# Where the text puts the mixers of a two-layer backbone: whole, or in pieces between products

## The chip, the cores and the metric

One core of one Trainium2 chip runs the whole program. The metric is the device time of one execution in microseconds.

## What is computed

Two streams of 256 tokens with 1024 features, a context (`c`) and the latents (`x`), pass through two layers. Each layer first mixes tokens and then channels:

```python
u_x = modulate(h_x, norm1[layer], sh1_x, sc1_x)
u_c = modulate(h_c, norm1[layer], sh1_c, sc1_c)
mix_c, mix_x = token_mixers(u_c, u_x, need_ctx, ...)   # w_in, four mixers, w_out
h_x = h_x + g1_x * mix_x
...
f = swiglu(flat, ...) if layer % 2 == 0 else moe_swiglu(flat, ...)
```

`token_mixers` multiplies by `w_in` (1024 x 2992), gives groups of columns to four mixers, concatenates their 4 x 256 output columns and multiplies by `w_out`. The mixers are windowed attention (A), the gated delta rule in both directions (B), latent attention (C) and retention (D). The latents read the context's keys, values and states; the context never reads the latents. In the last layer the context is only needed for those, so it has no output projection and no channel mixing there. Layer 0 has a dense SwiGLU of 3584 hidden units for both streams, layer 1 the top two of eight experts for the latents alone.

## The kernel before

Long products (input projection, output projection, channel mixing) are made exact by parts: a weight block is loaded to `raw` (five buffers), ScalarE rounds it to `hi` (L200, L225), VectorE takes the rest as `lo` (L201, L226), and TensorE (PE) runs three matmuls for each pair of blocks (`mm3`, L183 to L185, into the tile `acc`). Activations are split in the same way once. Weight loads are issued on SP's queue (L193 for blocks of 512 columns, L212 for blocks of 256, L287 for the modulation).

The kernel is written as a text in program order. For each engine the scheduler takes, of the instructions that are ready, the one that stands first in that text; `soon()` (L162) counts its instructions as 6000 places earlier, and is put around the splits of weights, around what empties the accumulators and around norms. Each engine then runs its own list in that order. Buffers of the mixers are single or double, named by tags, so a later user waits for the earlier one.

The functions that the change touches or that its steps pass through:

- `proj` (L1175) is a generator of the input projection. Its groups are `g` (delta rule: a group of 272 columns and three pairs of feature blocks, followed by the short convolution), `r` (retention: two groups of 512 columns), `a` (latent attention's 416 columns, then windowed attention's 512). For the latents of layer 0 the order is `rga`, a step for `r`, one for `g`, two for `a`.
- `gdn` (L938) is the delta rule. It transposes keys and values (L946), forms the systems of all chunks (L987 to L999), sends them to DRAM and back so that the 16 x 16 blocks on the diagonals lie a block to a partition (L1001, L1013), inverts these by forward substitution on VectorE (L1018 on), sends the inverses through DRAM again (L1026, L1034, L1035), and then takes four chunks, two steps in each of two directions, each with `inverse` (L1028) and `scan` (L1089). Chunks of one direction depend on each other through a state.
- `ret` (L749), `mla` (L641) and `swa` are retention, latent and windowed attention. The three of them share two PSUM banks (thread `AT`), so they follow each other. `attend` goes head by head: scores, maximum, exponential, transposes, sum, scaling into the tile `mix`.
- `outproj` (L1280) transposes `mix` (tile `mixt`, L1289) and multiplies by `w_out`; `add_residual` adds the gated result to the stream (tile `rtmp`, L373, and L374, for channel mixing partly on GpSimd).
- `ffn` (L1304) is a generator of dense channel mixing; each of its seven steps is a block of 512 hidden units. `tick` runs steps of the modulation's products between long products; `put_fill` queues such steps, `need_mod` runs them out.
- `load_stream` issues the two loads of a residual stream.

The decay tables of the delta rule (`gdn_decay`, with additions on GpSimd at L932) are made by the projection's last use of its first group, not by `gdn`. The order of the work around the change is that of the lines L1386 to L1423: first all four mixers of the context, then the latents' projection with the context's output projection in it, then all four mixers of the latents, then channel mixing of the context and of the latents; and in layer 1 the context's short projection, its delta rule, and the rest of the latents' channel mixing.

Of the kernel before, what the change touches and what calls it, by code (L numbers as in the profile page):

```python
# [17 lines left out]
PSUM = bass.MemoryType.PSUM  # L18
# [52 lines left out]
def bc(ap, pos, n):  # L71
    """Broadcast a new free dimension of n elements at position pos of the pattern."""
    a = list(ap.ap)
    a.insert(pos, [0, n])
    return bass.AP(tensor=ap.tensor, offset=ap.offset, ap=a)
# [3 lines left out]
def tile_backbone(ctx: ExitStack, tc: tile.TileContext, x, ctxs, cT, w_mod, w_in, w_out, w_q_up, w_kv_up,  # L79
# [42 lines left out]
    class Thread:  # L122
        """The rotating buffers of one strand of work."""
# [11 lines left out]
    class Long(Thread):  # L135
        """the strand of the long products: two pairs of banks take turns as accumulators,
        and what is short goes to the pair that is not at work"""
# [24 lines left out]
    def soon():  # L162
        """for what feeds the long matrix products"""
        return tc.high_priority(offset=6000)
# [22 lines left out]
    def slabs(w2d, nk, ranges, r0=0, ticks=(), calls=None):  # L187
        """Yields, for each block of 128 rows, the two exact parts of the columns in the ranges."""
        for a in range(0, nk, 2):
            r = raw.tile([128, 2, 512], F32, name="raw", tag="raw")  # L190
            w = 0
            for c0, c1 in ranges:
                nc.sync.dma_start(r[:, :, w:w + c1 - c0], w2d[r0 + a * 128:r0 + a * 128 + 256, c0:c1].rearrange(  # L193
                    "(k p) c -> p k c", p=128))
                w += c1 - c0
            for j in range(2):
                hi = spl.tile([128, 512], F32R, name="hi", tag="hi")
                lo = spl.tile([128, 512], F32R, name="lo", tag="lo")
                with soon():
                    S.copy(hi[:, :w], r[:, j, :w])  # L200
                    V.tensor_tensor(lo[:, :w], r[:, j, :w], hi[:, :w].bitcast(F32), op=OP.subtract)  # L201
                yield a + j, hi[:, :w], lo[:, :w]
            if a // 2 in ticks:
                tick()
            if calls and a // 2 in calls:
                calls[a // 2]()

    def halfslabs(w2d, nk, c0, ticks=()):
        """the same for 256 columns from c0"""
        for a in range(0, nk, 4):  # L210
            r = raw.tile([128, 2, 512], F32, name="raw", tag="raw")
            nc.sync.dma_start(r.rearrange("p a (b c) -> p (a b) c", c=256),  # L212
                              w2d[a * 128:a * 128 + 512, c0:c0 + 256].rearrange("(k p) c -> p k c", p=128))
            for j in range(2):
                hi = spl.tile([128, 512], F32R, name="hi", tag="hi")
                lo = spl.tile([128, 512], F32R, name="lo", tag="lo")
                with soon():
                    tsplit(hi, lo, r[:, j])
                for i in range(2):
                    yield a + j * 2 + i, hi[:, i * 256:i * 256 + 256], lo[:, i * 256:i * 256 + 256]  # L220
            if a // 4 in ticks:
                tick()
# [5 lines left out]
    class Parts:  # L228
        """feature-major activations [128, 8 blocks, 256 tokens] in two exact parts, a tile for two blocks"""

        def __init__(self, tags=None):
            """tags: buffers of mixers that aren't at work, in place of the own ones"""
            self.t, self.tags = [], tags
# [19 lines left out]
    def silu2(dst, src, n):  # L253
        """dst = 2 silu(src)"""
# [11 lines left out]
    # ---- residual streams  # L266
# [9 lines left out]
    # ---- modulation  # L276
# [26 lines left out]
    def bank0(name):  # L303
        """the banks that nothing else uses at the start"""
        turns.append(turns.pop(0))
        return turns[-1].ps(name)
# [22 lines left out]
    class Fill:  # L329
        """steps of the modulation that go between the long products"""  # L330
# [32 lines left out]
    def gate_tile(l, kind, s, factor, apart=False):  # L363
        """factor times a gate, along the columns of every partition"""
# [11 lines left out]
    # ---- modulated RMS norm, feature-major, in two exact parts  # L376
# [48 lines left out]
    # ---- rotary embedding of token-major heads: returns the two addends  # L425
# [18 lines left out]
    def put_mix(s, t, k0):  # L444
        """the 256 columns, from 128 k0, of the concatenated mixer outputs of a token tile"""
# [4 lines left out]
    # ---- softmax attention shared by the windowed and the latent mixers  # L450
    def attend(th, tp, s, t, score_fn, nk, v_fn, scale, sink, k0):
        """score_fn(h) -> PSUM scores [128, nk]; v_fn(h, kt) -> [128 keys, 64]; tp: thread of the transposes"""
# [32 lines left out]
    # ---- mixer A  # L485
# [57 lines left out]
    # ---- mixer C  # L543
    STC = {}

    def mla_in(l, s, full, c0):
        """c0: column of the key latent in the projected group (query latent at 0 when full)"""
# [103 lines left out]
    # ---- mixer D  # L651
    STD = {}

    def ret_tables(l):
# [11 lines left out]
        for h in range(4):  # L666
            # one of the two factors is 1 everywhere; both directions count on the diagonal
# [5 lines left out]
        # per token decays, [tile, head, direction]: of the context into its state, of the latents from it  # L673
# [16 lines left out]
    def ret_in(s, full):  # L690
        """keys and values"""
# [33 lines left out]
    def ret_qg(s):  # L725
        """queries and gates"""
# [67 lines left out]
    def gn_out(th, s, oc, g, k0):  # L794
        """oc: [128, 2 tiles x 4 heads x 64]; oc / rms(oc) times the gates"""
# [19 lines left out]
    # ---- mixer B  # L815
# [5 lines left out]
    # a [128, 128] matrix takes 128 rows of 128 and 128 more, which makes its blocks of 16 on the diagonal  # L821
    # and those of the matrix that follows equally spaced
    PAD = 128 * 129
    def mats(t, q):
        """the four matrices of a chunk, rows first"""
        return dram(t, [[128, 128], [PAD, 4], [1, 128]], q * 4 * PAD)

    def blocks(t, a, b):
        """the blocks of 16 on the diagonals"""
# [4 lines left out]
    def conv(l, sq, f, src):  # L834
        """short convolution over the tokens and twice silu of a block of 128 features"""
# [25 lines left out]
    def gdn_decay(l):  # L861
        """what follows from the decays and write strengths alone"""
        # decay and write strengths, [tile, direction, head]
# [29 lines left out]
        # running sums of the log decays, down the tokens and along the columns  # L893
# [44 lines left out]
    def gdn(l, s, full):  # L938
        sq = STB["sq"]
# [37 lines left out]
        # the systems of all chunks  # L977
# [25 lines left out]
        # inverses of all blocks of 16 on the diagonals, a block a partition [direction, tile, head, block]  # L1003
# [24 lines left out]
        def inverse(t, d, rs_):  # L1028
            """the transposed inverse of a chunk, from that of its blocks of 16"""
# [6 lines left out]
            # pairs of blocks of 16, all at once  # L1036
# [16 lines left out]
            # pairs of blocks of 32  # L1053
# [95 lines left out]
        class Res:  # L1149
            """the buffers of one chunk"""  # L1150
# [8 lines left out]
        for step in range(2):  # L1159
            for d in range(2):  # L1160
                t = step if d == 0 else 1 - step
# [8 lines left out]
    # ---- input projection, with each mixer's preparation  # L1170
# [4 lines left out]
    def proj(l, s, order, U=None, start=False):  # L1175
        """start: the first half of the contraction of the delta rule's groups comes ahead, in a step of its own"""
# [83 lines left out]
        def short_groups():  # L1260
            uses = gdn_gate(l, s, False), swa_in(s, False), mla_in(l, s, False, 0)

            def use(t, src):
                # keys and values of the windowed mixer, write strengths and decays, latents
# [14 lines left out]
    # ---- output projection and residual  # L1279
    def outproj(l, s, gt=None, then=None):  # L1280
        """gt: gates; without them, between other products, in the buffers of the delta rule"""
# [21 lines left out]
    # ---- dense channel mixing  # L1303
# [82 lines left out]
    gdn(0, "c", True)  # L1386
    ret(AT, "c")
    mla(AT, AT, "c")
    swa(AT, AT, 0, "c")
    load_stream("x")  # L1390
    g = proj(0, "x", "rga")
    for _ in range(3):
        next(g)
    outproj(0, "c")
    for _ in g:
        pass
    gdn(0, "x", True)
    ret(AT, "x")
    mla(AT, AT, "x")
    swa(AT, AT, 0, "x")  # L1400
    need_mod(0, 11)
    put_fill(1, range(12))
    g = ffn(0, "c")
    for _ in range(5):
        next(g)
# [11 lines left out]
    gdn(1, "c", False)  # L1417
    for _ in g:
        pass
# [4 lines left out]
    # ---- logits of the routed mixing: what the shift adds, and the tokens' part, whose norms come in afterwards  # L1424
# [50 lines left out]
    with soon():  # L1475
        gdn(1, "x", True)
# [24 lines left out]
    # ---- routed channel mixing  # L1501
# [47 lines left out]
    def route():  # L1549
        """the top two experts of each token, the lower index first among equals, and the tokens in two exact parts"""  # L1550
# [80 lines left out]
    def after(n, fn):  # L1631
        """fn after n more blocks of 128 rows of weights"""
# [9 lines left out]
    def pick(e, rnd):  # L1642
        """one-hot columns for the tokens of two experts; the ranks of those that they serve begin at -OFF"""
# [9 lines left out]
    def gather(oh, k2, vector=False):  # L1653
        """256 features of the tokens, feature-major and in two exact parts"""
# [20 lines left out]
    def back(oh):  # L1675
        """the way back to the tokens"""
# [19 lines left out]
    def turn(th, h2):  # L1696
        """the hidden units feature-major, in two exact parts"""
# [13 lines left out]
    def finish(prev, acc):  # L1711
        """the down product of a block of hidden units, and after the last the way back to the tokens"""
# [32 lines left out]
    def experts(rnd, X, ohT):  # L1745
        """the down product of a block of hidden units follows the next block's gate and up products;
        the splits of what lies between wait for some blocks of weights, which are split ahead of their products"""
# [46 lines left out]
    # ---- last norm  # L1794
    def weighted():
        """the sums of squares, and the stream times the weights of the norm"""
# [60 lines left out]
```

## Time and profile before

| | |
|---|---|
| median of 3 runs | 2356.82 us (2350.91 to 2360.22) |
| span of the profiled execution | 2352.2 us |
| PE, VectorE, ScalarE, GpSimd busy | 96%, 81%, 62%, 5% of the span |
| mean granted TensorE clock | 0.982 |
| moved by DMA | 579.53 MB, 246 GB/s on the mean |

The page gives the profiled execution's span; its own time has no other number there, and it lies inside the runs shown. In the trace, the context's delta rule runs from about 87 to 245 us and its windowed attention to 300 us; the latent mixers of layer 0 lie between 340 and 535 us; dense channel mixing of the context ends near 740 us, that of the latents near 1070 us, with the delta rule of layer 1's context between 846 and 966 us. The latents' mixers of layer 1 follow up to 1280 us, and from about 1340 us to the end the experts' weights stream in.

How to read the rows: PE is TensorE's matmul, PEld its weight load (the two overlap), DVE VectorE, ACT ScalarE, POOL GpSimd, SP the queue that issues most transfers. A name such as `acc<-uh,hi` is the written tile and what it is made from. "busy (x)" is busy time and, after the x, the number of instructions. A matmul's drawn length includes its way through the array, so that matmuls that follow each other overlap in the drawing.

### The profile page before, as it was taken

What the parts mean: (1) busy time and instruction counts of PE and PEld (TensorE: products, weight loads), DVE (VectorE), ACT (ScalarE), POOL (GpSimd) and SP (SyncE); (2) the same over time, 40 slices, a digit from 0 to 9 for tenths busy, and PEclk for the clock granted to TensorE, in tenths of its full rate; (3) what the DMA queues carried; (4) which work ended last, traced back from release to release, by engine and by line L of the source; (5) the groups of instructions that cost most, each with busy time, mean ns of one, the idle gap of its engine ahead of it and who ended that gap; (6) DMA issues with size and microseconds to landing.
All of it is one profiled execution on the core that took longest, in us unless ns stands there. A gap on an engine that the chain in (4) does not pass through costs nothing. (4 is left out here: it accounts for less than half of the span.)

```text
span 2352.2 us, 40101 instructions
## 1 busy us (share of the span) xinstructions
PE 2254.8 (96%) x14126; PEld 1846.9 (79%) x14126; DVE 1908.5 (81%) x4088; ACT 1458.0 (62%) x2887; POOL 119.3 (5%) x106
## 2 busy tenths in 40 slices
PE   6899999999999999999899899999999999999997
PEld 5668778889888888897677687887878787878785
DVE  5676888676787887678767799999998999988997
ACT  4443563344454464455345698988788888787786
POOL 0000100001211111110000000000000000000000
PEclk9899999999999999999899899999999999999999
DMA  8774554436666667565434599999999999999892
GB/s 297 218 223 119 167 170 146 122 118 215 222 209 213 204 193 225 155 189 147 134 104 154 206 379 347 356 338 341 357 355 337 344 366 342 366 322 362 316 374 103
DMA packets 363490, 579.53 MB, mean 246 GB/s; under 512 B 40864, under 2 KB 120976, under 8 KB 363280
## 3 DMA queue, kind: packets, MB, share of 16 engines
q1 hardware_dynamic: 361104, 568.50, 71.9%
q0 software_dynamic: 2176, 8.39, 1.0%
q8 instruction: 113, 1.85, 0.3%
q14 instruction: 97, 0.79, 0.1%
HBM read 568.37 MB, written 8.46 MB: 245 GB/s over the span
## 5 line engine op out<-in xcount | busy, mean ns | idle before, releaser
L1625 DVE TENSOR_TENSOR elo<-eraw,ehi 128x512 fp32r<-128x512 f32 x1344 | 839.3, 684 | 39.2 <-ACT ehi L1624 38.0
L1624 ACT CAST ehi<-eraw 128x512 fp32r<-128x512 f32 x1344 | 757.6, 622 | 47.7 <-PE gu L185 15.6
L200 ACT CAST hi<-raw 128x512 fp32r<-128x512 f32 (+3 forms) x408 | 244.9, 602 | 345.2 <-PE acc L185 180.4
L201 DVE TENSOR_TENSOR lo<-raw,hi 128x512 fp32r<-128x512 f32 (+3 forms) x408 | 305.3, 758 | 109.8 <-ACT hi L200 104.5
L183 PE MATMUL gu<-ehi,xhi 128*128 128x512 f32 x896 | 361.9, 404 | 1.4 <-ACT ehi L1624 1.2
L184 PE MATMUL gu<-elo,xhi 128*128 128x512 f32 x896 | 356.3, 398 | 1.2 <-DVE elo L1625 1.2
L185 PE MATMUL gu<-ehi,xlo 128*128 128x512 f32 x896 | 355.7, 397 | 0.0
L183 PE MATMUL acc<-uh,hi 128*128 128x256 f32 x1072 | 311.2, 291 | 3.4 <-DVE pl L882 2.4
L184 PE MATMUL acc<-ul,hi 128*128 128x256 f32 x1072 | 308.5, 288 | 0.0
L185 PE MATMUL acc<-uh,lo 128*128 128x256 f32 x1072 | 307.2, 287 | 0.5 <-DVE lo L201 0.3
L183 PEld LDWEIGHTS acc<-uh,hi 128*128 128x128 f32 x1072 | 206.3, 193 | 14.7 <-issue 11.5
L184 PEld LDWEIGHTS acc<-ul,hi 128*128 128x128 f32 x1072 | 207.0, 193 | 5.3 <-issue 4.3
L185 PEld LDWEIGHTS acc<-uh,lo 128*128 128x128 f32 x1072 | 206.7, 193 | 2.2 <-DVE lo L201 0.7
L183 PEld LDWEIGHTS gu<-ehi,xhi 128*128 128x128 f32 x896 | 168.3, 188 | 44.6 <-ACT ehi L1624 2.6
L184 PEld LDWEIGHTS gu<-elo,xhi 128*128 128x128 f32 x896 | 168.4, 188 | 44.0 <-DVE elo L1625 3.3
L185 PEld LDWEIGHTS gu<-ehi,xlo 128*128 128x128 f32 x896 | 168.3, 188 | 40.9 <-issue 1.7
L184 PE MATMUL pd<-elo,ehh 128*128 128x512 f32 x448 | 182.3, 407 | 0.0
L183 PE MATMUL pd<-ehi,ehh 128*128 128x512 f32 x448 | 177.2, 395 | 0.0
L185 PE MATMUL pd<-ehi,ehl 128*128 128x512 f32 x448 | 176.7, 395 | 0.0
L225 ACT CAST hi<-raw 128x512 fp32r<-128x512 f32 x156 | 96.4, 619 | 114.7 <-PE acc L184 100.3
L226 DVE TENSOR_TENSOR lo<-raw,hi 128x512 fp32r<-128x512 f32 x156 | 109.3, 701 | 54.0 <-ACT hi L225 52.9
L183 PE MATMUL acc<-hi,uh 128*128 128x512 f32 (+3 forms) x368 | 143.6, 399 | 8.6 <-ACT uh L225 5.4
(412 smaller groups left out, 3496.8 us busy)
## 6 DMA issues: line engine op xcount, KB each, us to landing
eraw<-md_dram SPq DMA_DIRECT2D x112, 1024.0 KB, 6.2
eraw<-mg_dram SPq DMA_DIRECT2D x108, 1024.0 KB, 7.0
eraw<-mu_dram SPq DMA_DIRECT2D x108, 1024.0 KB, 6.4
raw<-w_mod_dram SPq DMA_DIRECT2D x96, 512.0 KB, 4.2
raw<-fg_dram SPq DMA_DIRECT2D x56, 512.0 KB, 4.1
raw<-fu_dram SPq DMA_DIRECT2D x56, 512.0 KB, 4.6
raw<-fd_dram SPq DMA_DIRECT2D x56, 512.0 KB, 4.6
raw<-w_in_dram SPq DMA_DIRECT2D x50, 512.0 KB, 3.9
```

Source lines behind the costliest of these rows:

```text
L183: T.matmul(o_ap, lh, rh, start=start, stop=False, skip_group_check=skip)
L184: T.matmul(o_ap, lh, rl, start=False, stop=False, skip_group_check=skip)
L185: T.matmul(o_ap, ll, rh, start=False, stop=stop, skip_group_check=skip)
L200: S.copy(hi[:, :w], r[:, j, :w])
L201: V.tensor_tensor(lo[:, :w], r[:, j, :w], hi[:, :w].bitcast(F32), op=OP.subtract)
L225: S.copy(dst_hi, src)
L226: V.tensor_tensor(dst_lo, src, dst_hi.bitcast(F32), op=OP.subtract)
L1624: S.copy(hi, rr_[:, j])
L1625: V.tensor_tensor(lo, rr_[:, j], hi.bitcast(F32), op=OP.subtract)
```

## The change

`gdn` becomes a generator: a `yield` stands ahead of each of its four chunks, so that a first step makes everything up to the inverses of the diagonal blocks, and each further step one chunk (the last one also the end). The main program takes these steps, and the other mixers, between steps of `proj` and `ffn`:

- layer 0, context: preparation; `ret`; the latents' group `r`; two chunks; `mla`; two chunks; group `g`; `swa`; latent attention's group; output projection of the context; windowed attention's group. The latent stream's loads and the norm ahead of its projection stand earlier in the text.
- layer 0, latents: preparation; block 1 of the context's channel mixing; chunk; `ret`; block 2; chunk; `mla`; block 3; chunk; block 4; chunk; `swa`; block 5; output projection. `need_mod(0, 11)` and `put_fill(1, ...)` stand ahead of it.
- layer 1, context: preparation; block 3 of the latents' channel mixing; two chunks; block 4; two chunks; the last three blocks.

The delta rule of layer 1's latents is run as a whole, as before. No instruction's operands change. The diff also drops comments and docstrings; it is cut to the rest:

```diff
@@ -936,6 +936,7 @@
     def gdn(l, s, full):
...
         for step in range(2):
             for d in range(2):
+                yield
                 t = step if d == 0 else 1 - step
                 rs_ = res(d)
                 DT = inverse(t, d, rs_)
...
@@ -1383,26 +1385,43 @@
     put_fill(0, range(4, 12))
     for _ in g:
         pass
-    gdn(0, "c", True)
+    def rest(gen):
+        for _ in gen:
+            pass
+
+
+    load_stream("x")
+    d = gdn(0, "c", True)
+    next(d)
     ret(AT, "c")
+    g = proj(0, "x", "rga")
+    next(g)
+    next(d)
+    next(d)
     mla(AT, AT, "c")
+    rest(d)
+    next(g)
     swa(AT, AT, 0, "c")
-    load_stream("x")
-    g = proj(0, "x", "rga")
-    for _ in range(3):
-        next(g)
+    next(g)
     outproj(0, "c")
-    for _ in g:
-        pass
-    gdn(0, "x", True)
-    ret(AT, "x")
-    mla(AT, AT, "x")
-    swa(AT, AT, 0, "x")
+    rest(g)
     need_mod(0, 11)
     put_fill(1, range(12))
+    d = gdn(0, "x", True)
+    next(d)
     g = ffn(0, "c")
-    for _ in range(5):
-        next(g)
+    next(g)
+    next(d)
+    ret(AT, "x")
+    next(g)
+    next(d)
+    mla(AT, AT, "x")
+    next(g)
+    next(d)
+    next(g)
+    rest(d)
+    swa(AT, AT, 0, "x")
+    next(g)
     outproj(0, "x")
     layer_rows(1)
     ret_tables(1)
@@ -1414,14 +1433,19 @@
     next(g)
     c1 = proj(1, "c", "", uc)
     next(c1)
-    gdn(1, "c", False)
-    for _ in g:
-        pass
+    d = gdn(1, "c", False)
+    next(d)
+    next(g)
+    next(d)
+    next(d)
+    next(g)
+    rest(d)
+    rest(g)
     for _ in c1:
         pass
@@ -1473,7 +1497,7 @@
     with soon():
-        gdn(1, "x", True)
+        rest(gdn(1, "x", True))
     next(g)
```

## Rows read from the trace of the kernel before

**Rows 1.** The page: the span, and each engine's busy time (share of the span).
```profile
span 2352.2 us, 40101 instructions
...
PE 2254.8 (96%) x14126; PEld 1846.9 (79%) x14126; DVE 1908.5 (81%) x4088; ACT 1458.0 (62%) x2887; POOL 119.3 (5%) x106
```

**Rows 2.** Stretches: length, busy us (instructions) by engine, granted TensorE clock, DMA share, GB/s.
```profile
150.00:250.00 100.00, 95.51 (x932) 73.94 (x930) 70.94 (x237) 38.57 (x103) 0.00 (x0) 1.00 0.50 145
250.00:310.00 60.00, 55.73 (x413) 46.04 (x412) 50.39 (x179) 36.51 (x108) 6.65 (x12) 1.00 0.59 182
310.00:400.00 90.00, 86.19 (x542) 70.61 (x542) 72.61 (x211) 42.50 (x92) 0.00 (x0) 0.98 0.54 166
400.00:540.00 140.00, 137.33 (x1196) 113.91 (x1195) 96.65 (x272) 59.04 (x131) 12.01 (x8) 1.00 0.41 118
540.00:725.00 185.00, 183.71 (x1431) 163.76 (x1430) 138.56 (x229) 92.78 (x159) 24.30 (x17) 1.00 0.71 224
...
850.00:1000.00 150.00, 144.72 (x1315) 126.17 (x1314) 107.24 (x247) 67.94 (x138) 21.21 (x15) 0.99 0.64 195
1000.00:1070.00 70.00, 69.95 (x483) 64.89 (x482) 52.60 (x73) 36.27 (x62) 8.52 (x6) 1.00 0.61 183
...
1500.00:2000.00 500.00, 500.00 (x2211) 399.02 (x2210) 458.14 (x744) 411.59 (x753) 0.00 (x0) 1.00 0.98 349
```

**Rows 3.** PE's waits, 150 to 1000 us: total us, times, longest us.
```profile
PE cnt L604 <- DVE cn L594: 4.2, 2, 4.0
PE acc L183 <- DVE mrow L327: 3.0, 1, 3.0
PE pt L476 <- ACT p L467: 2.6, 3, 1.5
...
PE mixt L1289 <- DVE mlams L586: 0.8, 1, 0.8
```

**Rows 4.** Timeline of PE in channel mixing: start us, drawn us, instruction.
```profile
1032.28 0.39 PE L183 MATMUL acc<-hi,hh 128*128 128x512 f32 x1
1032.51 0.40 PE L184 MATMUL acc<-lo,hh 128*128 128x512 f32 x1
...
1033.09 0.28 PE L184 MATMUL acc<-ul,hi 128*128 128x256 f32 x1
1033.21 0.28 PE L185 MATMUL acc<-uh,lo 128*128 128x256 f32 x1
```

**Rows 5.** PE's products alone (tile acc), 150 to 250 us: PE busy.
```profile
150.00:250.00 100.00, 37.52 (x130) 1.00 0.50 145
```

**Rows 6.** Residual additions (tile rtmp) by stretch: length, DVE busy, POOL busy.
```profile
500.00:515.00 15.00, 2.65 (x4) 4.71 (x4) 1.00 0.51 157
...
552.00:562.00 10.00, 2.56 (x4) 4.70 (x4) 1.00 0.65 207
...
590.00:600.00 10.00, 2.56 (x4) 5.16 (x4) 1.00 0.69 225
...
625.00:663.00 38.00, 7.07 (x12) 5.94 (x4) 1.00 0.63 202
```

**Rows 7.** Windowed attention (tile sca) by stretch: PE, PEld, DVE, ACT busy.
```profile
250.00:275.00 25.00, 5.62 (x26) 3.59 (x26) 3.24 (x9) 2.81 (x10) 1.00 0.66 199
275.00:300.00 25.00, 4.46 (x22) 2.97 (x22) 2.00 (x6) 1.67 (x6) 1.00 0.51 156
300.00:325.00 25.00, 0.00 (x0) 0.00 (x0) 0.28 (x1) 0.00 (x0) 1.00 0.51 168
```

**Rows 8.** Transposes ahead of the output projection (tile mixt): PE, PEld, DVE, ACT.
```profile
293.00:310.00 17.00, 2.89 (x16) 1.89 (x16) 2.75 (x4) 2.34 (x4) 1.00 0.47 154
```

**Rows 9.** Timeline of SP at the context's first inverses.
```profile
182.59 1.16 SPq L1034 DMA_DIRECT2D DD<-invd  x2
```

**Rows 10.** SP's waits, 75 to 540 us.
```profile
SPq L287 <- DVE DD L1071: 21.8, 2, 11.7
```

**Rows 11.** Timeline of SP: the second load of the latent stream.
```profile
52.95 0.46 SPq L274 DMA_DIRECT2D h_x<-x_dram  x1
```

More of the change, by code (lines that the diff above doesn't have):

```diff
@@ L1385, in tile_backbone @@
         pass
-    gdn(0, "c", True)
+    def rest(gen):
+        for _ in gen:
+            pass
+    load_stream("x")
+    d = gdn(0, "c", True)
+    next(d)
     ret(AT, "c")
+    g = proj(0, "x", "rga")
+    next(g)
+    next(d)
+    next(d)
     mla(AT, AT, "c")
+    rest(d)
+    next(g)
     swa(AT, AT, 0, "c")
-    load_stream("x")
-    g = proj(0, "x", "rga")
-    for _ in range(3):
-        next(g)
+    next(g)
     outproj(0, "c")
-    for _ in g:
-        pass
-    gdn(0, "x", True)
-    ret(AT, "x")
-    mla(AT, AT, "x")
-    swa(AT, AT, 0, "x")
+    rest(g)
     need_mod(0, 11)
     put_fill(1, range(12))
+    d = gdn(0, "x", True)
+    next(d)
     g = ffn(0, "c")
-    for _ in range(5):
-        next(g)
+    next(g)
[10 more added lines that the diff above has]
+    next(g)
     outproj(0, "x")
```

## The prediction

> **What bounds the kernel now.** I read the page's totals first: the matrix engine (PE) is drawn busy for 96% of the span, DVE for 81% [rows 1]. Next came the table of stretches, where the span falls into parts with different limits [rows 2]. In the routed stage, from 1350 us on, PE is drawn busy without a gap (500.00 of 500) and the 16 DMA engines are at 0.98; nothing of the change lies there, so whatever the earlier part gains or loses should arrive at the end unshortened. In the two stretches that hold products alone (540 to 725 and 1000 to 1070) PE idles 1.29 of 185 us and 0.05 of 70. In the stretches where mixers lie among the products it idles more: 4.49 + 4.27 us between 150 and 310 (context mixers), 3.81 + 2.67 between 310 and 540 (latent mixers of layer 0 with the first two blocks of channel mixing), 5.28 between 850 and 1000 (delta rule of layer 1's context). The list of what PE waited for there shows many short waits with different causes and only a few of 3 to 4 us [rows 3]: no transfer and no single engine is the limit. So the kernel is bound by PE's work, and the mixed stretches leak a few per cent of their time.
>
> "Busy" is generous. In a stretch of products alone a 128x512 product starts 0.23 us after the one before and a 128x256 product 0.12 us, but they are drawn as 0.39 and 0.28 long [rows 4]. A gap of up to 0.16 us after each is thus hidden inside busy time, and the idle sums above are lower bounds of what leaks.
>
> **The change, part by part.** No operation is added or removed: the same instructions are written down in another order, and the scheduler takes, of what is ready on an engine, what stands first in the text (splits and evictions under `soon` 6000 places earlier). So the sum of the work stays, and only the idle time can move.
>
> 1. Context mixers, layer 0. Before, all four stand ahead of every product of the latent projection. After, the order is: delta rule's preparation, retention, the retention group (96 products), two chunks of the delta rule, latent attention, two more chunks, the delta rule's group, windowed attention, the rest. In the trace the mixers crowd together: between 150 and 250 us only 130 of PE's 932 matmuls belong to products [rows 2, 5]. Reachable idle time, 150 to 310: 4.49 + 4.27 = 8.8 us [rows 2].
>
> 2. Latent mixers, layer 0. Before, all ahead of five blocks of channel mixing; the second block's residual additions lie between 500 and 515 us, beside the mixers' end, and the next three blocks' follow from 552, 590 and 625 us without a mixer beside them [rows 6]. After, each piece stands between two blocks. Reachable: 3.81 + 2.67 = 6.5 us [rows 2].
>
> 3. Delta rule of layer 1's context, now in pieces between blocks of the latent channel mixing. Reachable: 5.3 us [rows 2].
>
> Together 20.6 us over 160 + 230 + 150 = 540 us. The nearest row for what remains after spreading is 540 to 725: 1.29 / 185 = 0.7%, or 3.8 us in 540. That gives 16.8 us. Bounds: nothing (the same small waits go along with the mixers wherever they stand), and twice this, 33 us, since the drawn busy time hides gaps. I take 16.8, between the two and the only one of them that a row counts.
>
> 4. What it costs. Windowed attention of the context now stands behind the delta rule's group: 48 products of 272 columns, priced as 256 columns (0.12 us), and 144 of 256 columns, 192 x 0.12 = 23 us [rows 4]. Its chain runs from 250 to 300 us, 10.1 us of PE in about 50, with none of its matmuls before or after [rows 7]. Behind it wait the output projection of the context (its transposes lie between 293 and 310, right at the chain's end [rows 8]), the context's stream, its norm, and with that every product of the channel mixing. If all 23 us of the group are still to do when latent attention ends, the chain is delayed by that and later has too little beside it; if the group is done, by nothing. Bounds 0 and 18 us (worked out under the rivals). The idle rate of 250 to 310, where the same chain runs among the same products, is 4.27 / 60 = 7%; on some 41 us (23 + 18) it makes 2.9 us. I take 3.
>
> 5. Queues. Each delta rule carries 18 DMA issues on SP (4 systems out, 2 blocks in, 4 inverses out, 8 matrices in), three times 54, all moved behind weight loads of some product groups. They take some 0.6 us each to issue [rows 9], 11 us of SP per delta rule, spread over 60 us or more. The number stays; a load of matrices that waits for its buffer holds the modulation's weight load behind it in SP's queue for up to 11.7 us already now [rows 10], and PE's list of waits shows no trace of it [rows 3]: the raw buffers cover it. I cost this at nothing; without that cover it is those 12 us, once per delta rule. POOL carries residual additions of the channel mixing and the additions to the decay tables; the latter are issued by the projection, not by the delta rule, and are not moved. The two loads of the latent stream stand earlier in the text but were already issued early, the second at 53 us [rows 11]: nothing. The refilled modulation steps stand earlier too, but no product lies between the old place and the new: nothing.
>
> 6. The end of the latent mixers. Windowed attention of the latents stands before the fifth block, and the output projection behind it. If it is late, two more blocks of the context, some 38 us each in the trace (552 to 590 [rows 6]), stand ready to fill PE. Nothing.
>
> Sum: -16.8 + 3 = -13.8, rounded -14 us. The profiled execution has a span of 2352.2 us [rows 1]; 2352.2 - 14 = 2338. The median shown is 4.6 us above that span, so I forecast 2338 + 5 = 2343 us, 0.6% below the median. What a measurement of this kernel can tell from no change is about 0.5%, or 12 us: the forecast lies just outside.
>
> **Rivals.**
> A. Order by readiness already mixes them. The scheduler had the products to hand all along, and the text only ranks what is ready. For it: in the densest stretch, 400 to 540, PE idles only 2.67 of 140 us with mixers in front [rows 2]. Against it: that 310 to 400 and 850 to 1000 idle 4 and 3.5%. Time: 2357, give or take 6.
>
> B. Slower: windowed attention of the context becomes the gate. Its place is between latent attention and the context's output projection. Condition: the delta rule's group is used up before the attention begins, which it may be, as the group now ranks above it. Then the chain of 50 us [rows 7] has beside it its own 10 us of PE and two groups of the latent projection, 48 products each at no more than 0.23 us, 22 us together [rows 4]. 50 - 10 - 22 = 18 us stand empty, and the products that bridge the context's norm later are spent too. Time: 2357 + 18 = 2375. For it: PE already waits here for the attention's last result (0.8 us at `mixt` [rows 3]). Against it: the next delta rule's preparation can fill some of it.
>
> C. More than the idle rows show. Small gaps hidden inside the drawn busy time vanish as well. In 1000 to 1070 weight loads fill 64.89 / 70 = 92.7%; in the three mixed stretches 75.0, 80.2 and 84.1% [rows 2]. Brought up to 92.7%, that is 28 + 29 + 13 = 70 us; half of it gives 2357 - 35 = 2322. Against it: in the routed stage, which runs 512-column products alone and without a gap, the same share is 399.02 / 500 = 79.8% [rows 2]; the share depends on the shapes, and the mixed stretches hold many of that shape. The Trainium skill (Perfetto Trace Analysis, Identifying the Most-Contended Engine) says that matmul busy time is no measure of how near TensorE is to its limit and that the busy share of LDWEIGHTS should be read in its place; by that rule this rival's 70 us would be the headroom, where the idle rows give 21. The rows of the routed stage speak against the size by that rule.
>
> **How the numbers follow.** Forecast 0.45, A 0.25, B 0.18, C 0.07, something else 0.05. Of the forecast's share 0.36 lie beyond 12 us of gain and 0.09 within; of A 0.19 within and 0.03 on each side; of B 0.14 beyond and 0.04 within; C is all gain; the rest 0.01, none and 0.04. Faster 0.47, same 0.32, slower 0.21. The range takes in the forecast with its bounds (twice the gain at no cost: 2357 - 33 = 2324; gain nothing: 2360), A, and B to a little past its price, and leaves out most of C: 2318 to 2378.
>
> **What would show it.** Right: PE idle below 2% between 150 and 310 us and below 1.5% between 310 and 540; mixers' rows spread over blocks two to five of the context's channel mixing; the routed stage's full rate starting some 14 us earlier. Step 4 shows in windowed attention's rows ending after 300 us and in what PE waits for between then and the first channel mixing products. Wrong: the same waits at the same size (A); PE idle of 10 us or more around 280 to 340 us (B); a rise of the LDWEIGHTS share well beyond the fall of the idle time (C).

## The result, and the profile after

The changed kernel took 2390.48 us (median of 4 runs, 2387.84 to 2397.59) against 2356.62 us before: a ratio of 1.0141, 95% interval 1.0104 to 1.0179. It is 34 us slower; 2343 us and a range up to 2378 had been forecast. The times of one kernel move with the clock that was granted to TensorE (its mean was 0.982 in the profiled execution before and 0.969 after); what that means for the comparisons below stands at the end.

The page after, against [rows 1]:

```profile
span 2389.9 us, 40114 instructions
...
PE 2278.2 (95%) x14126; PEld 1867.3 (78%) x14126; DVE 1907.5 (80%) x4088; ACT 1457.3 (61%) x2887; POOL 118.0 (5%) x106
```

The number of matmuls and the busy time of VectorE and ScalarE are the same to a promille: no work was added. Where the 38 us of span come from is seen by dating the same event in both traces: the end of a stage's last multiplication by the gate (L373), which the residual addition itself follows within 3 us. For the context's output projection, before and after (start, length, instruction):

```profile
336.18 1.28 DVE L373 TENSOR_TENSOR rtmp<-acc,gate 128x512 f32<-128x512 f32 x2
```
```profile
368.97 1.28 DVE L373 TENSOR_TENSOR rtmp<-acc,gate 128x512 f32<-128x512 f32 x2
```

By this event the context's output projection ends at 337.5 us before and at 370.3 after (+32.8), channel mixing of the context at 738.7 and 775.0 (+36.3), that of the latents at 1068.5 and 1109.8 (+41.3); the program ends at 2352.2 and 2389.9 (+37.7). So 33 us are lost ahead of 370 us, and everything later gives or takes a few.

The stretches of the kernel after (columns as in [rows 2]), first up to the scores of the context's windowed attention, then from them to the end of the products beside it (296 us), then to its last head, then the two stretches that answer to 250 to 337 and 337 to 739 before:

```profile
150.00:264.00 114.00, 112.63 (x1108) 90.27 (x1107) 79.92 (x261) 46.93 (x123) 0.00 (x0) 1.00 0.60 176
264.00:296.00 32.00, 25.20 (x136) 22.43 (x135) 27.45 (x81) 15.05 (x42) 6.43 (x12) 0.79 0.37 119
296.00:336.00 40.00, 24.76 (x77) 15.31 (x76) 13.88 (x55) 12.59 (x46) 0.00 (x0) 0.56 0.08 26
```
```profile
264.00:370.00 106.00, 83.18 (x347) 62.59 (x347) 62.36 (x202) 45.17 (x126) 6.43 (x12) 0.74 0.28 91
370.00:775.00 405.00, 398.36 (x3112) 341.38 (x3111) 295.81 (x675) 182.20 (x352) 39.66 (x28) 0.99 0.57 175
```

And of the kernel before, cut at the same events:

```profile
250.00:337.00 87.00, 82.73 (x531) 65.86 (x531) 68.11 (x233) 52.39 (x145) 6.65 (x12) 1.00 0.58 180
337.00:739.00 402.00, 392.70 (x3114) 337.73 (x3112) 301.75 (x675) 183.90 (x352) 40.11 (x28) 1.00 0.57 176
```

Up to 264 us the changed kernel is as dense as hoped (PE idles 1.2% of 114 us; it was 4.5% between 150 and 250). Then follow 72 us in which PE gets 213 matmuls: by 296 us the work is used up but for the attention, and the attention goes one step at a time. Its tile by stretch, against [rows 7], where 26 and 22 matmuls lay in the first two rows and none in the third:

```profile
250.00:275.00 25.00, 0.70 (x2) 0.29 (x2) 0.00 (x0) 0.00 (x0) 0.98 0.49 137
275.00:300.00 25.00, 0.96 (x6) 0.82 (x6) 0.68 (x2) 0.55 (x2) 0.75 0.37 128
300.00:325.00 25.00, 10.10 (x30) 6.56 (x28) 3.28 (x10) 2.83 (x10) 0.52 0.07 21
325.00:340.00 15.00, 4.81 (x14) 2.94 (x13) 1.70 (x5) 1.13 (x4) 0.50 0.00 0
```

Two scores are made at 264 us, and the next matmuls on this tile come 35 us later. What held the first head up stands in the queues of VectorE and ScalarE. The timelines of PE, VectorE and ScalarE, for the first head of the kernel after (scores, maximum, exponential, transposes, copy of the transposes):

```profile
263.76 0.70 PE L535 MATMUL sca<-kTa,qTa 64*128 64x256 f32 x2
...
281.31 0.42 DVE L461 TENSOR_REDUCE mxv<-sca 128x1 f32<-128x256 f32 x1
...
282.98 0.46 ACT L467 ACTIVATE p<-sca,nms 128x256 f32<-128x256 f32 x1
...
283.59 0.44 PE L476 MATMUL pt<-cs,p 128*128 128x128 f32 x2
...
298.63 0.35 ACT L478 COPY pT<-pt 128x256 f32<-128x256 f32 x1
```

and of the kernel before:

```profile
250.01 0.70 PE L535 MATMUL sca<-kTa,qTa 64*128 64x256 f32 x2
250.75 0.42 DVE L461 TENSOR_REDUCE mxv<-sca 128x1 f32<-128x256 f32 x1 [0.27 <-PE sca L535]
251.90 0.47 ACT L467 ACTIVATE p<-sca,nms 128x256 f32<-128x256 f32 x1
253.06 0.37 ACT L478 COPY pT<-pt 128x256 f32<-128x256 f32 x1 [0.51 <-PE pt L476]
```

What took 3 us before takes 35: the maximum comes 17 us after the scores, the copy 15 us after the transposes. VectorE's groups between 264 and 296 us after the change show what it does instead:

```profile
L842 DVE SCALAR_TENSOR_TENSOR y<-acc,cl,y 128x254 f32<-128x254 f32 (+1 forms) x18 | 8.6, 476 | 0.1
L201 DVE TENSOR_TENSOR lo<-raw,hi 128x416 fp32r<-128x416 f32 (+1 forms) x10 | 7.3, 740 | 4.2 <-ACT hi L200 4.2
L257 DVE SCALAR_TENSOR_TENSOR sqkv<-th,y 128x256 f32<-128x256 f32 x5 | 2.1, 424 | 0.1
```

That is the convolution behind the delta rule's group of the latent projection, and the splits of the next group's weights. ScalarE's groups in the same stretch:

```profile
L200 ACT CAST hi<-raw 128x416 fp32r<-128x416 f32 (+1 forms) x10 | 5.4, 553 | 9.7 <-PE acc L185 7.7 <-PE acc L184 2.0
L934 ACT ACTIVATE ET<-ET,ngc 128x128 f32<-128x128 f32 x10 | 3.5, 397 | 0.0
```

The copy thus stands behind roundings of the next groups' weights, which themselves waited 9.7 us for PE, and behind the exponentials of the delta rule's decay tables (L934). ScalarE was not full; what its list held ahead of the copy was not ready. When all this is done the products are done as well, and seven heads run alone, some 5 us each, from 300 to 335 us.

### The profile page after: what moved, and what is told of

Read it like the earlier page. It is cut to its first block, busy times and chain, and to the rows that moved or that the text cites. A ratio compares the mean times of both kernels' runs of the same rounds, so it can differ in the third digit from the quotient of the medians.

```text
span 2389.9 us, 40114 instructions
## 1 busy us (share of the span) xinstructions
PE 2278.2 (95%) x14126; PEld 1867.3 (78%) x14126; DVE 1907.5 (80%) x4088; ACT 1457.3 (61%) x2887; POOL 118.0 (5%) x106
## 5 line engine op out<-in xcount | busy, mean ns | idle before, releaser
L184 PE MATMUL acc<-lo,uh 128*128 128x512 f32 (+3 forms) x368 | 145.8, 397 | 5.7 <-DVE lo L201 5.7
```

Source lines behind the costliest of these rows:

```text
L184: T.matmul(o_ap, lh, rl, start=False, stop=False, skip_group_check=skip)
```

## The experiments

Each run shared a chip with runs of the kernel before, and its ratio is to those; their medians there were 2358 to 2363 us, so the times below are not to be set against 2356.62. Times of one kernel spread more on those chips, and intervals of half a per cent can hide the few us that were forecast, so the dated events of the profiled execution carry the verdicts.

**Which of the three places.** Each of the first three runs keeps one part of the change and puts the other two back (`rest(gdn(...))`, then the mixers, as before; the early loads of the latent stream stay).

> Only the context mixers of layer 0 in pieces; the other two places as before. Theory (the context's windowed attention, now behind the delta rule's group, runs with no product beside it): the whole loss comes from here, 2356 + 33 = 2389 us, with the first residual additions of the context's output projection near 369 us in place of 336. Rival 1 (the pieces cost the same everywhere, through more switching between mixers and products): about a third of the loss, 2368 us.

Measured: 2388.17 us, ratio 1.0135 (1.0042 to 1.0228); the context's output projection ends at 362.3 us, the program at 2387.2. By its time the whole loss is here. At the output projection it is 25 us, not the 33 that I expected; channel mixing of the context ends at 771.1, 32 us late, after 409 us at a clock of 0.97 (401 us at 1.00 before).

> Only the latent mixers of layer 0 in pieces between blocks of the context's channel mixing. Theory: nearly nothing, 0 to +3 us (the end of the output projection of the latents moved by 36 us after the change, of which 33 were there already before these mixers), so 2356 to 2360. My own forecast of the recorded text had a gain of some 5 us here: 2351. Rival 1: 2368.

Measured: ratio 1.0009 (0.9972 to 1.0045). A third of the loss is not here. The gain of 5 us that I forecast lies within this interval; the events below speak against it.

> Only the delta rule of layer 1's context in pieces between blocks of the latents' channel mixing. Theory: +6 us (the lag behind the kernel before grows from 35 to 41 us over these blocks), so 2362. The recorded forecast had a gain of some 4 us: 2352. Rival 1: 2368.

Measured: ratio 1.0008 (0.9956 to 1.0060). The interval holds both the 6 us of loss that I expected and the 4 us of gain that I had forecast. The stretch itself, the latents' channel mixing, tells more: here, before, and in the changed kernel,

```profile
740.00:1070.00 330.00, 321.26 (x2619) 288.13 (x2620) 248.33 (x517) 159.49 (x312) 43.70 (x30) 0.99 0.63 192
```
```profile
739.00:1068.00 329.00, 321.09 (x2619) 287.87 (x2619) 248.13 (x517) 159.91 (x312) 43.73 (x30) 0.99 0.63 193
```
```profile
775.00:1110.00 335.00, 325.31 (x2622) 292.07 (x2623) 248.73 (x518) 159.49 (x313) 43.58 (x30) 0.98 0.62 189
```

From event to event these are 330.4, 329.8 and 334.8 us: at the same clock the pieces change nothing, and the 5 us by which the lag grew over these blocks in the changed kernel go with its lower clock.

The same holds for the latents' part: between the end of the context's output projection and the end of its channel mixing PE's idle time falls from 9.3 us of 402 to 6.6 of 405 after the change, yet the stretch is 3 us longer, at a clock of 0.99 in place of 1.00. A run below that has these pieces too (the attention under `soon()`) kept the clock at 1.00 there:

```profile
342.00:742.00 400.00, 393.29 (x3116) 338.28 (x3114) 295.93 (x676) 182.28 (x353) 40.22 (x28) 1.00 0.58 177
```

PE idles 6.7 us, and from event to event the stretch takes 400.2 us against 401.2 before. So 2.6 us less idle time are worth 1 us at most, not the 5 that I forecast for this part.

**One line.** In the changed kernel only the context's windowed attention is moved:

```diff
     rest(d)
+    swa(AT, AT, 0, "c")
     next(g)
-    swa(AT, AT, 0, "c")
     next(g)
```

> The changed kernel with one line moved: the context's windowed attention ahead of the delta rule's group of the latent projection, right behind the delta rule. Theory: the 33 us come back, 2390 - 33 = 2357 us, and PE between 290 and 340 us is busy with products again. Rival 2 (what delays the attention is the retention group and the chunks ahead of latent attention, so the attention begins late anyhow): at most 10 us come back, 2380 us or more.

Measured: ratio 1.0039 (0.9995 to 1.0083); the output projection ends at 340.7 us, 3 us behind the kernel before in place of 33:

```profile
339.38 1.28 DVE L373 TENSOR_TENSOR rtmp<-acc,gate 128x512 f32<-128x512 f32 x2
```

Rival 2 falls. With all context mixers in pieces but the attention early, PE idles 10.8 us between 150 and 341 us, at a clock of 0.96, where it was 8.8 between 150 and 337 at 1.00 before: no gain shows from the pieces of the context either.

The reverse: the kernel before, all mixers whole, with that one line moved back behind the two groups (the loads of the latent stream stay early here and in the two later runs on the kernel before; the diff is cut to the order of the rest).

```diff
     mla(AT, AT, "c")
-    swa(AT, AT, 0, "c")
     g = proj(0, "x", "rga")
-    for _ in range(3):
-        next(g)
+    next(g)
+    next(g)
+    swa(AT, AT, 0, "c")
+    next(g)
```

> The kernel before (its mixers whole) with one move: the context's windowed attention behind the retention and the delta rule's groups of the latent projection, its place in the changed text. Theory (its place in the text is the cause): most of the loss, 2380 to 2390 us, and a stretch between attention and the end of the context's output projection with some 350 matmuls in 100 us or more, as against 531 in 87. Rival 2 (it takes the pieces too: chunks ahead of and behind latent attention): under 2365 us.

Measured: 2392.15 us, ratio 1.0106 (1.0061 to 1.0152); the output projection ends at 366.4 us. Its end, and the stretch from the attention's first scores to there:

```profile
365.15 1.28 DVE L373 TENSOR_TENSOR rtmp<-acc,gate 128x512 f32<-128x512 f32 x2
```

```profile
257.00:366.00 109.00, 90.15 (x473) 69.34 (x473) 68.44 (x221) 51.65 (x142) 6.33 (x12) 0.80 0.40 127
```

109 us, and more matmuls than I expected in them (473, not 350), but 29 of the 33 us are there without a single piece. The pieces are not needed for the loss.

**Do products beside the attention help?** After the change SP holds one weight load for 41 us while the weights of the output projection sit in the raw buffers:

```profile
SPq L193 <- DVE rope L439: 41.3, 1, 41.3
```

I took this for the reason why the last group of the latent projection does not run beside the attention.

```diff
     next(g)
-    outproj(0, "c")
     rest(g)
+    outproj(0, "c")
```

> The changed kernel with one exchange: the last group of the latent projection (windowed attention's, 48 products of 512 columns) ahead of the context's output projection. Theory with its second half (the weight loads of the output projection sit in the raw buffers and SP holds the last group's loads behind them for 41 us, so the last products that could run beside the attention don't): the 48 products, 48 x 0.23 = 11 us, move beside the attention and 8 to 11 us come back, 2380 us. If the loads aren't what keeps them away: 2390 us, no change.

Measured: 2409.8 us, ratio 1.0156 (1.0043 to 1.0268). The products do move, and nothing is won:

```profile
263.00:371.00 108.00, 90.36 (x404) 67.63 (x404) 70.79 (x223) 50.81 (x141) 6.43 (x12) 0.83 0.35 109
```

404 matmuls in place of 347, and the output projection ends at 370.9 us as after the change (370.3). Channel mixing of the context then ends at 776.3, not earlier: with 11 us of products done ahead, the time behind the projection is as long as it was. The gain that I expected did not come; the other branch, no change, has the ratio right (1.0156 against 1.0141, not told apart) and its reason wrong, since the products did move. What they left behind shows right after the projection, in this run and after the change:

```profile
371.00:400.00 29.00, 24.98 (x161) 22.25 (x162) 22.47 (x74) 10.03 (x23) 0.00 (x0) 0.76 0.22 67
```
```profile
370.00:400.00 30.00, 29.19 (x202) 24.77 (x202) 28.09 (x79) 15.28 (x35) 0.00 (x0) 1.00 0.40 118
```

There the last group had kept PE busy while the context's norm, ahead of channel mixing, was made. Without it PE idles 4.0 of 29 us at a clock of 0.76, where it idled 0.8 of 30 at 1.00. What was filled on one side of the projection was opened on the other.

> The kernel before with the last group of the latent projection ahead of the context's output projection. A try at a better version: if the attention still lacks products in the kernel before (PE idles 4.3 of 60 us there), 2 to 4 us are gained, 2353 us; if the last group is needed later, to bridge the context's norm ahead of channel mixing, 5 to 10 us are lost, 2364 us.

The same exchange in the kernel before: 2372.14 us, ratio 1.0045 (1.0006 to 1.0083); the output projection ends at 355.7 us, 18 later, and channel mixing of the context at 752.5, 14 later: the products done ahead give back 4 of the 18 us, with the clock at 0.81 between 356 and 400 us. The second branch of the expectation holds, as in the run above: the last group is needed later. No better version.

**Place or rank, and on which engine.** The attention stays where the change put it, but ranks earlier.

```diff
-    swa(AT, AT, 0, "c")
+    with soon():
+        swa(AT, AT, 0, "c")
```

> The changed kernel with the context's windowed attention left where it stands in the text but under soon(), so that it ranks ahead of the delta rule's group. Theory (rank, and with it the order on PE, VectorE and ScalarE, is the cause): like the run with the line moved, 2357 to 2362 us. Rival 3 (what matters is which buffers are handed out first, which follows the text and not the rank): 2380 to 2390 us.

Measured: ratio 1.0030 (0.9974 to 1.0085); the output projection ends at 341.5 us, 29 of the 33 us earlier. It is the rank, not the place.

Then the rank of its VectorE and ScalarE instructions alone, and that of its matmuls alone (in `attend`, the statements of one kind stand under `soon()` for this call):

> The changed kernel; of the context's windowed attention only the VectorE and ScalarE instructions stand under soon(), its matmuls keep their rank. Theory, as sharpened by the trace (between 264 and 296 us the first head's maximum waits on VectorE behind the convolution and splits of the delta rule's group, its copy on ScalarE likewise): most of the loss comes back, 2360 to 2368 us, first maximum within 5 us of its scores. Rival (the attention waits for its turn on PE, behind the products): no more than 5 us come back, 2385 us.

> The changed kernel; of the context's windowed attention only the matmuls stand under soon(). Theory: little comes back, 2383 to 2390 us. Rival (its turn on PE): 2360 us.

Measured: VectorE and ScalarE alone, ratio 1.0031 (0.9994 to 1.0068), output projection at 349.3 us, program at 2363.8; matmuls alone, 1.0134 (1.0094 to 1.0174), 358.4 us and 2386.8:

```profile
347.91 1.39 DVE L373 TENSOR_TENSOR rtmp<-acc,gate 128x512 f32<-128x512 f32 x2
```
```profile
357.12 1.28 DVE L373 TENSOR_TENSOR rtmp<-acc,gate 128x512 f32<-128x512 f32 x2
```

The maxima (tile `mxv`, two VectorE instructions for each of the eight heads) of the first:

```profile
270.00:282.00 12.00, 1.25 (x4) 0.88 0.29 89
282.00:300.00 18.00, 1.88 (x6) 0.51 0.19 58
300.00:325.00 25.00, 1.88 (x6) 1.00 0.38 128
```

and of the second, whose first head has its maximum at 250 us, ahead of these rows:

```profile
270.00:282.00 12.00, 0.61 (x2) 0.69 0.18 64
282.00:300.00 18.00, 0.59 (x2) 0.88 0.53 178
300.00:325.00 25.00, 3.19 (x10) 0.50 0.04 15
```

With its matmuls first the attention starts at 245 us, 19 earlier, and still has most of its maxima after 300 us; the second head's scores wait from 255 to 277 us for theirs. With its VectorE and ScalarE work first it starts at 269, 5 us later than after the change, as its matmuls have kept their rank, but the first maximum follows its scores by 2 us and the heads then go through at 4 to 7 us each. So VectorE's and ScalarE's queues weigh more (21 of the 33 us come back at the output projection) than PE's (12). The two are not shares of one sum: lifted together, in the run before, they give 29. The two queues were not told apart from each other. In the times, the 12 us of the second run do not show: its latent channel mixing took 348 us at a clock of 0.94, where it was 329 at 0.99 before.

**A try at more.** The kernel before with the same `soon()` around that attention.

> A try at a better version: the kernel before with the context's windowed attention under soon(). If its chain (50 us from 250 us on in the kernel before) is still held up by the convolution, the context's output projection ends up to 8 us earlier than at 337.5 us; the total gains at most the idle time around it, 2352 to 2357 us at the same granted clock.

Measured: ratio 1.0025 (0.9977 to 1.0074); the output projection ends at 334.9 us, 2.6 earlier, and nothing of it is left in the time. No run of this study beats the kernel before.

## Why the prediction was wrong

**The frame held.** The kernel is bound by PE's work up to the routed stage, and what was lost at 370 us arrived at the end (+33 there, +38 at the end).

**The gain of 16.8 us did not come.** The step that failed is the reading of the idle rows as recoverable time. Parts 2 and 3, measured alone, make no difference within 0.6%, and the stretches themselves are closer: part 2 is worth 1 us at most (400.2 us in place of 401.2, with 2.6 us less idle time), part 3 nothing (330.4 in place of 329.8). Part 1 without the displaced attention ends the output projection 3 to 4 us later, not 8.8 earlier. My lower bound, nothing, was the right one.

**Step 4 was mis-sized: 3 us taken, 33 measured, outside its own bounds of 0 and 18.** I had the right place (windowed attention, behind the delta rule's group, ahead of the output projection) and, as rival B, the right sign and consequence, at 18 us and a chance of 0.18. Two terms of it were wrong. First, I priced the group above the attention by its products on PE, 23 us. What holds the attention more is what hangs on those products, the convolution, the decay tables and the splits of the next weights on VectorE and ScalarE, which stand ahead of its maxima and copies: the run that lifts only that part of the attention gets 21 us back, the one that lifts only its matmuls 12. Second, I let the attention's chain keep its 50 us and filled it with 22 us of the latents' last two groups. The first head, begun at 264 us, took until 300, and seven of the eight heads came when the group and all that hangs on it were done. The two groups were no help: latent attention's had run by 296 us, and the last one, when brought forward by hand, was missing behind the projection.

**The idle rate of 7% that gave the 3 us** came from a stretch in which the attention ranked ahead of the products. It says what a chain costs that is served early, not one that is served last.

**Step 5 held for the queues of transfers**, which cost nothing that the runs show: with the last group ahead, the one long wait on SP (41 us) shrinks to 6.7 us and the output projection ends no earlier. Its remark that the decay tables are not moved missed something: they stayed with their group, but the attention moved behind them, and their exponentials (L934) are among what its first copy stands behind. **Step 6 held** as far as a time can tell: the run with the latents' part alone, which has that end in it, is no slower.

**Rival A** fits what parts 2 and 3 did: the pieces make no difference there. That it is readiness which mixes them was not shown by itself. **Rival C** is not borne out by any run. Weight loads fill 152.86 of 220 us, 69%, between 150 and 370 us after the change:

```profile
150.00:370.00 220.00, 195.81 (x1454) 152.86 (x1453) 142.29 (x461) 92.10 (x248) 6.43 (x12) 0.88 0.45 135
```

which is less than the 75% before, since PE stood still. By the Trainium skill's rule (Perfetto Trace Analysis, Identifying the Most-Contended Engine) the share should tell the headroom; here it followed the loss, and the 70 us that rival C worked out from it were not found by any order tried.

## What to carry to other kernels

When a latency chain is put behind a block of throughput work in a scheduler's text, count what that block puts on every engine that the chain passes through, above all the work that was given priority because it feeds the matmuls. Ask of each chain what cannot begin before its end: a chain that gates the next stage's supply of products belongs ahead of the work that could be done beside it, and filler that is moved to it is missing where it stood. An idle share that is spread over many small waits need not be time that an order can win back (here 2.6 us less idle time gave 1 us at most); test it on one stretch before adding up all.

## What the runs showed of the hardware that I had not expected

The same program took between 2347.8 and 2400.8 us in 75 executions of the kernel before, and the granted clock explains nearly all of it: a straight line, 2310.5 + 2160 x (1 - clock) us, leaves 2.0 us of scatter. A line of a similar slope (1918 to 2240) fits each of the other kernels that had ten executions; read at a clock of 0.98 the kernel before stands at 2354 us, the latents' part alone at 2356, layer 1's part alone at 2354, the attention moved ahead at 2358, both runs with its VectorE work lifted at 2355, the kernel before with `soon()` at 2353 and with the last group ahead at 2359. The two that keep most of the gap stand higher, at 2366 (the attention alone moved back) and 2363 (its matmuls alone lifted). For these the line is no correction, since part of their low clock lies in the gap itself. One stretch where executions differ can be seen: the delta rule of layer 1's context in the run with the latents' part alone, and in the kernel before, between 950 and 1000 us:

```profile
950.00:1000.00 50.00, 50.00 (x408) 41.55 (x408) 21.48 (x53) 13.78 (x32) 6.25 (x4) 0.76 0.31 95
```
```profile
950.00:1000.00 50.00, 50.00 (x449) 44.27 (x446) 33.30 (x68) 21.59 (x40) 6.77 (x5) 1.00 0.54 167
```

PE is drawn fully busy in both, with the clock at its lower level (1.2 in place of 2.4 GHz) for half of the one. It had fallen at 930 us, right behind a wait of PE of 1.4 us for a load of the delta rule's inverses (0.5 us in the kernel before, where it stayed up), and rose at 974 us. In the changed kernel the gap itself lies mostly at the lower level: 0.56 between 296 and 336 us. That is not what begins the loss: the first head stands in line from 264 us on, up to 296 us at a clock of 0.79. But the attention's own matmuls run slower in the gap. The values of the first head, then scores, transposes and values of the last:

```profile
299.04 0.66 PE L481 MATMUL sca<-va,pT 128*128 128x64 f32 x4 [3.01 <-ACT pT L478]
...
330.10 1.22 PE L535 MATMUL sca<-kTa,qTa 64*128 64x256 f32 x2
332.74 0.69 PE L476 MATMUL pt<-cs,p 128*128 128x128 f32 x2 [1.42 <-ACT p L467]
333.95 1.12 PE L481 MATMUL sca<-va,pT 128*128 128x64 f32 x4 [0.52 <-ACT pT L478]
```

Against the first head's 0.70, 0.44 and 0.66 that is 1.2 us more a head; over the last six heads, which wait for each of these steps, that is an estimate of 7 us. The first products behind the gap run slowly for 5 us. So some 7 to 10 of the 33 us, an estimate, may be the clock's. Whether the loss would be smaller at the full clock was not tried.
